# Conditioning bursts that wait for a fp32 product bundle, in one decoder layer on one core

## The chip, the cores and the metric

One core of one Trainium2 chip. The metric is device time in microseconds of one execution of the whole kernel. Engines are named as in the profile: PE is TensorE's matmuls (PEld its weight loads), DVE VectorE, ACT ScalarE, POOL GpSimd, SP the engine that issues most loads.

## What is computed

One layer (DEPTH is 1) of a conditioned decoder, for a prompt of 256 tokens and 8 samples of 8 tokens, 320 rows in all that share every weight. Cut to what matters here:

```python
mod = silu(c) @ w_ada + b_ada                      # conditioning: 6 sections of 2048
sh1, sc1, g1, sh2, sc2, g2 = split(mod, 6)
h = rmsnorm(x) * (1 + sc1) + sh1
q, k, v, og, u, ga, gb, alr = split(h @ w_in)
loga = log_sigmoid(alr @ w_a2 + b_a) / 16
o, s_new = gla(q, k, v, loga, s0)                  # recurrence, 4 heads, chunked
y_a = rmsnorm(o, gla_norm_g) * silu(og)
y_b = pool(u) * pool_scale                         # causal averages, then w_pool
x = x + g1 * ((sigmoid(ga) * y_a + sigmoid(gb) * y_b) @ w_o)
h2 = rmsnorm(x) * (1 + sc2) + sh2
x = x + g2 * ((silu(gate) * up) @ w_down)          # gate, up = split(h2 @ w_gu)
```

and a final norm. All weights and activations are fp32.

## The kernel before

**Projections.** Activations lie transposed, 16 tiles of 128 channels by 320 rows, each split into a high and a low part of a reduced fp32 kind (`hh`/`hl` ahead of the recurrence, `mh`/`ml` ahead of `w_o`). A weight tile is loaded (`raw`), its high part cast by ACT (`whi`, L160) and its low part taken by DVE (`wlo`, L161); five buffers of each. `mm3` then issues three matmuls: `whi` with the high part (L199), `whi` with the low part (L200), `wlo` with the high part (L201). I call these three a *step*. `proj` computes 256 columns in four *chunks* of four channel tiles, eight steps a chunk, 32 steps a *unit*. Units stand in two rotating accumulators (`ps`).

**Two kinds of other work stand between chunks.** At the end of each chunk `proj` calls two pumps.

- `ada_pump` adds a rate to a counter and, when it reaches one, calls `ada_step`: a *conditioning burst* of 32 fp32 matmuls (L252), each writing 32 of the 128 output partitions (a 32-column tile), with four loads of `w_ada` ahead and the next four behind. Every second burst ends a group: ACT copies it out (`adasb`), PE transposes it, DVE adds the bias. The rate is one burst in six chunks during the recurrence (24 in all up to the end of w_o), and about one in four during w_o.
- `gla_pump` does the same with `queue`, the list of the recurrence's *bundles* for the head whose projections have just been made. A bundle is a few functions of `gla_steps` called in one go (`together`): `s_gk` (gate products, fp32, L779/L780), `s_exp` (running sums, reduced fp32, L810/L811), `s_nat2`, `s_nat3`, `s_kp` (transposes), `s_attP` (sample scores, fp32, L955), `s_inter` (sample state read, fp32, 32-column tiles, L979), `s_state` (L1000), `s_att` (prompt scores, fp32, 32-column tiles, L879, and the 128-wide L884), `s_o` (L933/L935), `s_sfin` (L944), `s_norm` (column sum of squares, fp32, L1016, then root on ACT, reciprocal and scaling on DVE).

After the last head's bundles, `merge_step` gates the norm's result and adds the pooled branch (DVE, L1122 and L1123), `hilo` splits it into `mh12` to `mh15` (ACT) and `ml12` to `ml15` (DVE), and the w_o units read them in their fourth chunk. The units' first three chunks read only heads 0 to 2.

**What sets the order.** The code is written in one order; the compiler's scheduler then orders each engine's instructions by its own model of time, within the data's dependences and a few pinned places. The order of each engine is fixed before the run, and each engine works strictly in its order. So a call that moves in the code moves rows of several engines, some of them far away.

Of the kernel before, what the change touches and what calls it, by code (L numbers as in the profile page):

```python
# [82 lines left out]
def body(tc, A):  # L83
# [15 lines left out]
    def nm(s):  # L99
        uid[0] += 1  # L100
        return "%s_%d" % (s, uid[0])

    def misc():
        return pmisc.tile([P, 512], F32, tag="m", name=nm("pm"))
# [30 lines left out]
    def tr_exact(out, in_):  # L135

        PE.matmul(out, lhsT=in_, rhs=identr, start=True, stop=True)  # L137
# [44 lines left out]
    def split_chunk(src, nk, nn, key=None):  # L182

        if key in ready:
            k = 0
            for e in ready.pop(key):
                for j in range(e.h.shape[1]):
                    yield k, e.h[:, j], e.l[:, j]
                    k += 1
            return  # L190
        raw = asked.pop(key) if key in asked else raw_chunk(src, nk, nn)
        step = 512 // nn
        for k in range(0, nk, step):
            hi, lo = split(raw[:, k:min(k + step, nk)])
            for j in range(hi.shape[1]):
                yield k + j, hi[:, j], lo[:, j]

    def mm3(ps, whi, wlo, xhi, xlo, start, stop):
        PE.matmul(ps, lhsT=whi, rhs=xhi, start=start, stop=False)  # L199
        PE.matmul(ps, lhsT=whi, rhs=xlo, start=False, stop=False)  # L200
        PE.matmul(ps, lhsT=wlo, rhs=xhi, start=False, stop=stop)  # L201

    def proj(w, col, k0, k1, xh, xl):

        ps = pmain.tile([P, 2, 512], F32, tag="pm", name=nm("ps"))
        for c0 in range(k0, k1, 4):
            nk = min(4, k1 - c0)
            for j, whi, wlo in split_chunk(w[:, c0:c0 + nk, col:col + 256], nk, 256, (col, c0) if w is win else None):
                kt = c0 + j
                for i in range(2):  # L210
                    mm3(ps[:, i, :T], whi[:, i * P:(i + 1) * P], wlo[:, i * P:(i + 1) * P],
                        xh[kt], xl[kt], kt == k0, kt == k1 - 1)
            ada_pump()
            gla_pump()
        return ps

    def projs(wcols, k0, k1, xh, xl):
# [93 lines left out]
    ada_done = []  # L311
    ada_acc = [0.0, 0.0, 0]
# [2 lines left out]

        ada_acc[:] = [0.0, rate / 4, limit]

    def ada_pump():
        ada_acc[0] += ada_acc[1]
        if ada_acc[0] >= 1.0 and len(ada_done) < ada_acc[2]:  # L320
            ada_acc[0] -= 1.0
            ada_step()

    queue = []
    gla_acc = [0.0, 0.0]

    def gla_pump():

        gla_acc[0] += gla_acc[1]
        while gla_acc[0] >= 1.0:  # L330
            gla_acc[0] -= 1.0
            if queue:
                queue.pop(0)()

    def modp(sec, kt):
        return mod[:, sec * KT + kt, 0:1]
# [423 lines left out]
    def gla_steps(g):  # L760
# [3 lines left out]
        st = []  # L764
# [39 lines left out]
        def s_exp(d):  # L804
            def f():
                pa, pb = misc(), misc()
                ds = slice(d * P, (d + 1) * P)
                for ps, rows, s, rhs, a, b in ((pa, P, 0, M0, 0, NM0), (pa, TS, 2, MS, NM0, NM0 + NMS),
                                               (pb, P, 1, M1, 0, NM1)):
                    PE.matmul(ps[:, a:b], lhsT=E["lgh"][:rows, s, ds], rhs=rhs, start=True, stop=False)  # L810
                    PE.matmul(ps[:, a:b], lhsT=E["lgl"][:rows, s, ds], rhs=rhs, start=False, stop=True)  # L811
                EQ, EK, EX = E["EQ"][:, d], E["EK"][:, d], E["EX"][:, d]
                i16 = 1.0 / 16.0
                for dst, sc in ((EQ, i16), (EK, -i16)):
                    S.activation(dst[:, 0:P], pa[:, 0:P], AF.Exp, scale=sc)
                    S.activation(dst[:, P:2 * P], pb[:, 0:P], AF.Exp, scale=sc)
                    S.activation(dst[:, TP:T], pa[:, NM0:NM0 + TS], AF.Exp, scale=sc)
                S.activation(EX[:, 0:144], pa[:, P:NM0], AF.Exp, scale=i16)
                S.activation(EX[:, 144:416], pb[:, P:NM1], AF.Exp, scale=i16)
                S.activation(EX[:, 416:480], pa[:, NM0 + TS:NM0 + 2 * TS], AF.Exp, scale=i16)  # L820
            return f
# [142 lines left out]
        def s_load(gg, d):  # L964
            def f():
                t = lp.tile([P, 4, DV], F32, tag="S0", bufs=2, name=nm("S0"))
                nc.gpsimd.dma_start(t, A["state_gla"][0, 4 * gg:4 * gg + 4, h, d * P:(d + 1) * P, :]
                                    .rearrange("b p e -> p b e"))
                E["S0", gg, d] = t
            return f  # L970

        def s_inter(gg):
            def f():
                pt = E["oi"] = misc()
                PE.matmul(pt, lhsT=attP[:, gg], rhs=E["vp"][:, gg], start=True, stop=False,
                          skip_group_check=True)
                for d in range(2):
                    for j in range(4):
                        PE.matmul(pt[32 * j:32 * j + 32, :], lhsT=qeP[:, d, 4 * gg + j, :], rhs=E["S0", gg, d][:, j],  # L979
                                  start=False, stop=d == 1, tile_position=(0, 32 * j), skip_group_check=True)  # L980
            return f

        def s_oback(gg):
            def f():
                t = lp.tile([P, DV], F32, tag="sf", name=nm("osn"))
                S.copy(t, E["oi"])
                p2 = misc()
                for e in range(4):
                    tr(p2[:, e * P:(e + 1) * P], t[:, e * P:(e + 1) * P])
                src = p2.rearrange("p (e j t) -> p e j t", e=4, t=32)  # L990
                for e in range(4):
                    V.tensor_copy(s3(E["o"][:, e, TP + 32 * gg:TP + 32 * gg + 32]), src[:, e, :, 0:LS])
            return f
# [29 lines left out]
        def together(*fs):  # L1023
            def f():
                for x in fs:
                    x()
            return f

        def states(gg, d):
            return s_state(gg, d, 0), s_state(gg, d, 2)  # L1030

        st += [together(s_load(0, 0), s_load(0, 1), s_wa2), s_gk, together(s_exp(0), s_exp(1)),
               together(s_prod, s_vstack), together(s_nat2, s_nat3, s_kp(0)), s_attP, s_inter(0),
               together(s_oback(0), *states(0, 0), s_load(1, 0)), together(*states(0, 1), s_load(1, 1), s_att),
               together(s_nat, s_kp(1)), together(s_o(0), s_o(1), s_sfin(0), s_sfin(1)), s_inter(1),
               together(s_oback(1), *states(1, 0)), together(*states(1, 1)), s_norm]
        return st, E

    def pool_steps(g):
# [96 lines left out]
    st, E = gla_steps(g0)  # L1136
# [13 lines left out]
    for h in range(1, H):  # L1150
        g = new_group(h)
        for kind, i, col in units(h):
# [8 lines left out]
            if kind == "u":  # L1161
                pump(len(queue))
                st, E = gla_steps(g)
# [277 lines left out]
```

## Time and profile before

| what | value |
|---|---|
| median of 3 runs | 1951.73 us (1951.36 to 1951.95) |
| the profiled execution, own time | 1950.37 us |
| its span, first to last instruction | 1948.6 us |
| mean granted TensorE clock | 0.997 |
| TensorE busy | 1929.4 us, 99% |
| VectorE, ScalarE busy | 1015.9 us, 824.1 us |
| conditioning bursts from the recurrence to the end of w_o | 24 of 32 matmuls |

A row of the timeline gives the start (us from the span's start), the duration, the engine, the source line, what is written and read, and how many instructions were merged into the row. An fp32 instruction of TensorE shows as two records, so a burst of 32 reads x64. Matmuls overlap: a duration of 0.31 says little, and the distance from one start to the next is what a matmul costs. In the rows of stretches, each engine's busy time is followed by the granted clock (1.00 is full), the DMA share and GB/s.

### The profile page before, as it was taken

To read this page: it belongs to the slowest core of one execution; us is meant where nothing else is said; L and a number is where in the kernel's file an instruction comes from. 1 tells how busy PE (TensorE), PEld (TensorE's weight loads), DVE (VectorE), ACT (ScalarE), POOL (GpSimd) and SP (SyncE) were. 2 spreads that over 40 slices of the span, in tenths; PEclk is the share of its full clock that TensorE was granted. 3 is DMA by queue.
4 is the path that set the end of the run, shared out by engine and by line. 5 is a ranking of instruction groups with operands and counts; after the bars stand their busy time and mean duration, and the time that the engine had idled before them with its cause. 6 is when DMAs were issued, how large, how long until landed. Compare 5 with 4: busy or idle time off the path is not lost.

```text
span 1948.6 us, 37288 instructions
## 1 busy us (share of the span) xinstructions
PE 1929.4 (99%) x15060; PEld 1851.4 (95%) x15060; DVE 1015.9 (52%) x1909; ACT 824.1 (42%) x1482; POOL 135.8 (7%) x255
## 2 busy tenths in 40 slices
PE   9999999999999999999999999999999999999997
PEld 7899999899899989889999999999999999999997
DVE  3566565565466437666574444444444444444554
ACT  4333355355336333744353333343333334344443
POOL 1012210121002002010020000000000000000000
PEclk9999999999999999999999999999999999999998
DMA  9988555686786778589656655444444444444443
GB/s 323 398 275 266 191 167 173 228 294 212 272 272 203 228 260 279 179 288 327 222 188 207 218 189 178 152 146 152 146 153 151 152 152 152 148 148 149 150 137 103
DMA packets 324608, 400.84 MB, mean 206 GB/s; under 512 B 13546, under 2 KB 264682, under 8 KB 324098
## 3 DMA queue, kind: packets, MB, share of 16 engines
q1 hardware_dynamic: 312082, 357.95, 56.5%
q0 software_dynamic: 12272, 40.25, 5.8%
q8 instruction: 118, 1.93, 0.4%
q14 instruction: 56, 0.45, 0.1%
q10 hardware_dynamic: 80, 0.26, 0.0%
HBM read 373.96 MB, written 24.67 MB: 205 GB/s over the span
## 4 chain that ended last, share of the span: by engine, by line
PE 92%; DVE 1%; DMA 1%; ACT 0%; issue 0%; DVEq 0%; ACTq 0%
PE ps L199 28%; PE ps L200 27%; PE ps L201 27%; PE pm L252 4%; PE pm L979 1%; PE pm L1000 1%; PE pm L944 1%; PE pm L133 1%; DMA raw<-w_in 1%; PE pm L933 0%; PE pm L810 0%; PE psy L199 0%; PE pm L137 0%; PE psy L200 0%; PE psy L201 0%
## 5 line engine op out<-in xcount | busy, mean ns | idle before, releaser
L161 DVE TENSOR_TENSOR wlo<-raw,whi 128x512 fp32r<-128x512 f32 x948 | 652.7, 692 | 751.6 <-ACT whi L160 749.3
L160 ACT CAST whi<-raw 128x512 fp32r<-128x512 f32 x948 | 583.8, 620 | 936.2 <-PE ps L200 864.7
L199 PE MATMUL ps<-hh,whi 128*128 128x320 f32 x1408 | 443.8, 316 | 2.5 <-ACT hh L585 1.0
L200 PE MATMUL ps<-hl,whi 128*128 128x320 f32 x1408 | 437.0, 311 | 0.7 <-DVE hl L601 0.7
L201 PE MATMUL ps<-hh,wlo 128*128 128x320 f32 x1408 | 436.6, 310 | 0.1
L200 PE MATMUL ps<-h2l,whi 128*128 128x320 f32 x1408 | 434.8, 309 | 0.8 <-DVE h2l L1291 0.8
L199 PE MATMUL ps<-h2h,whi 128*128 128x320 f32 x1408 | 435.2, 310 | 0.0
L201 PE MATMUL ps<-h2h,wlo 128*128 128x320 f32 x1408 | 434.8, 309 | 0.0
L199 PEld LDWEIGHTS ps<-hh,whi 128*128 128x128 f32 x1408 | 264.7, 188 | 22.7 <-issue 15.3
L200 PEld LDWEIGHTS ps<-hl,whi 128*128 128x128 f32 x1408 | 265.0, 188 | 4.5 <-issue 1.8
L201 PEld LDWEIGHTS ps<-hh,wlo 128*128 128x128 f32 x1408 | 265.0, 188 | 1.9 <-issue 0.9
L199 PEld LDWEIGHTS ps<-h2h,whi 128*128 128x128 f32 x1408 | 264.1, 188 | 1.6 <-ACT ah L348 1.4
L200 PEld LDWEIGHTS ps<-h2l,whi 128*128 128x128 f32 x1408 | 264.3, 188 | 1.1 <-DVE h2l L1291 1.1
L201 PEld LDWEIGHTS ps<-h2h,wlo 128*128 128x128 f32 x1408 | 264.3, 188 | 0.0
L201 PE MATMUL ps<-ah,wlo 128*128 128x320 f32 x704 | 218.1, 310 | 0.0
L200 PE MATMUL ps<-al,whi 128*128 128x320 f32 x704 | 217.6, 309 | 0.0
L199 PE MATMUL ps<-ah,whi 128*128 128x320 f32 x704 | 217.5, 309 | 0.0
L199 PEld LDWEIGHTS ps<-ah,whi 128*128 128x128 f32 x704 | 132.2, 188 | 0.0
L201 PEld LDWEIGHTS ps<-ah,wlo 128*128 128x128 f32 x704 | 132.2, 188 | 0.0
L200 PEld LDWEIGHTS ps<-al,whi 128*128 128x128 f32 x704 | 132.2, 188 | 0.0
L252 PE MATMUL pm<-raw,scT 128*32 128x128 f32 (+1 forms) x2688 | 95.9, 290 | 0.0
L252 PEld LDWEIGHTS pm<-raw,scT 128*32 128x32 f32 x2688 | 72.7, 110 | 17.1 <-issue 9.2
(327 smaller groups left out, 1565.6 us busy)
## 6 DMA issues: line engine op xcount, KB each, us to landing
raw<-w_ada SPq DMA_DIRECT2D x192, 512.0 KB, 7.4
raw<-w_gu SPq DMA_DIRECT2D x176, 512.0 KB, 3.5
raw<-w_in SPq DMA_DIRECT2D x173, 512.0 KB, 4.2
raw<-w_down SPq DMA_DIRECT2D x79, 512.0 KB, 3.3
S<-state_gla POOLq DMA_DIRECT2D x16, 1024.0 KB, 8.1
o_gs<-S POOLq DMA_DIRECT2D x16, 1024.0 KB, 6.1
raw<-w_o SPq DMA_DIRECT2D x32, 512.0 KB, 6.3
raw<-w_down SPq DMA_DIRECT2D x15, 256.0 KB, 2.5
```

What stands on the lines that cost most here:

```text
L133: PE.transpose(out, in_, ident[:k, :k])
L160: S.copy(hi, raw)
L161: V.tensor_sub(lo, raw, hi.bitcast(F32))
L199: PE.matmul(ps, lhsT=whi, rhs=xhi, start=start, stop=False)
L200: PE.matmul(ps, lhsT=whi, rhs=xlo, start=False, stop=False)
L201: PE.matmul(ps, lhsT=wlo, rhs=xhi, start=False, stop=stop)
L252: ins = PE.matmul(ps[32 * j:32 * j + 32, 0:w], lhsT=scT[:, k, :], rhs=raws[j], start=k == 0 if start is None else start, stop=k == KT - 1 ...
L944: PE.matmul(pt, lhsT=E["kdn"][:, s, d * P:(d + 1) * P], rhs=E["vn"][:, s], start=s == 0, stop=s == 1)
L979: PE.matmul(pt[32 * j:32 * j + 32, :], lhsT=qeP[:, d, 4 * gg + j, :], rhs=E["S0", gg, d][:, j], start=False, stop=d == 1, tile_position=(0 ...
L1000: PE.matmul(pt, lhsT=kpz[:, j, d * P:(d + 1) * P], rhs=E["vp"][:, gg], start=True, stop=True)
```

## The change

Four edits, all in what is issued when; no arithmetic changes.

- At the end of a chunk `proj` calls `gla_pump` ahead of `ada_pump`.
- A burst that is due while `queue` holds bundles waits until it is three chunks late, unless a bundle marked as ending in an fp32 product is issued: then it is issued directly behind that bundle (`ada_due`, `full`, `last`).
- Nine of the fifteen bundles are marked so.
- Two bundles are turned round, so that they end in fp32 transposes: `s_nat2, s_kp(0), s_nat3` and `s_kp(1), s_nat`.

```diff
             gla_pump()
             ada_pump()
-            gla_pump()
...
+    def ada_due(late):
+        if ada_acc[0] >= 1.0 + late * ada_acc[1] and len(ada_done) < ada_acc[2]:
+            ada_acc[0] -= 1.0
+            ada_step()
+
     def ada_pump():
         ada_acc[0] += ada_acc[1]
-        if ada_acc[0] >= 1.0 and len(ada_done) < ada_acc[2]:
-            ada_acc[0] -= 1.0
-            ada_step()
+        ada_due(3 if queue else 0)
...
             if queue:
-                queue.pop(0)()
+                step = queue.pop(0)
+                step()
+                if step in full:
+                    ada_due(0)
...
-               together(s_prod, s_vstack), together(s_nat2, s_nat3, s_kp(0)), s_attP, s_inter(0),
+               together(s_prod, s_vstack), last(together(s_nat2, s_kp(0), s_nat3)), last(s_attP), last(s_inter(0)),
...
-               together(s_oback(1), *states(1, 0)), together(*states(1, 1)), s_norm]
+               together(s_oback(1), *states(1, 0)), together(*states(1, 1)), last(s_norm)]
```

Lines behind the first edits shift by 9 to 13: L1016 of before is L1025 in the changed file, L879 is L888, L933 is L942, L1018 is L1027.

In the order of TensorE, of the bursts issued while a head's bundles are pending or just done, three stand directly behind or among 32-column products before and three in the change; behind 128-wide fp32 products or transposes one before, six in the change. Three places are shown, with row names as the order gives them.

First, TensorE around the norm's column sum of head 3, in w_o (ps_1592 is unit 1, ps_1568 unit 0, mh3 a tile of head 0, mh11 the last of head 2, mh12 the first of head 3). Before:

```order
L199 MATMUL ps_1592_10098<-mh3_9846,whi_1596_10117 128x320
L1016 MATMUL pm_1559_9784<-acc_1557_9777,cst_76 128x320
L200 MATMUL ps_1592_10098<-ml3_9862,whi_1596_10117 128x320
L201 MATMUL ps_1592_10098<-mh3_9846,wlo_1597_10118 128x320
L199 MATMUL ps_1592_10098<-mh3_9846,whi_1596_10117 128x320
```

and in the change:

```order
L200 MATMUL ps_1592_10098<-ml11_9870,whi_1612_10230 128x320
L1025 MATMUL pm_1554_9743<-acc_1552_9736,cst_76 128x320
L201 MATMUL ps_1592_10098<-mh11_9854,wlo_1613_10231 128x320
L252 MATMUL pm_1555_9751<-raw_1501_9464,scT_86 32x128 x8
L252 MATMUL pm_1555_9751<-raw_1500_9462,scT_86 32x128 x8
L252 MATMUL pm_1555_9751<-raw_1499_9460,scT_86 32x128 x8
L252 MATMUL pm_1555_9751<-raw_1498_9458,scT_86 32x128 x8
L199 MATMUL ps_1568_9947<-mh12_9855,whi_1585_10052 128x320
L199 MATMUL ps_1592_10098<-mh12_9855,whi_1615_10248 128x320
L200 MATMUL ps_1568_9947<-ml12_9871,whi_1585_10052 128x320
```

The sum stood 16 steps, a burst and a transpose ahead of the first row that reads mh12; now one projection matmul and a burst stand between.

Second, ScalarE at the same place: weight splits (whi), the table load and root of the norm, and the casts of head 3's merged tiles (mh). Before:

```order
L160 CAST whi_1607_10196<-raw_1604_10178 128x512
L1018 ACT_TABLE_LOAD
L1018 ACTIVATE acc_1557_9777<-pm_1559_9784,epst_81 128x320
L160 CAST whi_1610_10214<-raw_1609_10212 128x512
L305 COPY adasb_1602_10173<-pm_1537_9665 128x128
```

and in the change:

```order
L160 CAST whi_1617_10264<-raw_1614_10246 128x512
L160 CAST whi_1625_10299<-raw_1624_10297 128x512
L1027 ACT_TABLE_LOAD
L1027 ACTIVATE acc_1552_9736<-pm_1554_9743,epst_81 128x320
L357 CAST mh12_9855<-mg3_114 128x320
```

All weight splits that units 0 and 1 need, and one of unit 2 (whi_1625), now stand ahead of the root, and nothing between the root and the cast of mh12.

Third, TensorE at head 0's output products (v_15 are the values, transposed into pm_636 and copied by ACT into w4_635). Before:

```order
L199 MATMUL ps_649_4255<-hh4_95,whi_657_4302 128x320
L200 MATMUL ps_649_4255<-hl4_1197,whi_657_4302 128x320
L933 MATMUL pm_643_4230<-attT_3226,w4_634_4176 128x256
L935 MATMUL pm_643_4230<-attT_3226,w4_634_4176 128x128
L933 MATMUL pm_643_4230<-attT_3226,w4_634_4176 128x256
```

and in the change:

```order
L133 MATMUL pm_628_4138<-identr_78,adasb_627_4136 128x128
L137 MATMUL pm_634_4176<-identr_78,w4_537_3601 128x128 x2
L133 MATMUL pm_636_4184<-identr_78,v_15_250 128x128 x4
L133 MATMUL pm_637_4190<-identr_78,v_15_250 128x128 x4
L942 MATMUL pm_643_4230<-attT_3226,w4_635_4183 128x256
L942 MATMUL pm_644_4236<-attT_3226,w4_635_4183 128x256
L199 MATMUL ps_649_4255<-hh0_91,whi_651_4258 128x320
```

The first output products moved up to directly behind the transposes whose copy they read.

More of the change, by code (lines that the diff above doesn't have):

```diff
@@ L212, in proj @@
                         xh[kt], xl[kt], kt == k0, kt == k1 - 1)
+            gla_pump()
             ada_pump()
-            gla_pump()
         return ps
@@ L316, in ada_rate @@
         ada_acc[:] = [0.0, rate / 4, limit]
+    def ada_due(late):
+        if ada_acc[0] >= 1.0 + late * ada_acc[1] and len(ada_done) < ada_acc[2]:
+            ada_acc[0] -= 1.0
+            ada_step()
     def ada_pump():
         ada_acc[0] += ada_acc[1]
-        if ada_acc[0] >= 1.0 and len(ada_done) < ada_acc[2]:
-            ada_acc[0] -= 1.0
-            ada_step()
+        ada_due(3 if queue else 0)
     queue = []
     gla_acc = [0.0, 0.0]
+    full = []
     def gla_pump():
@@ L1030, in states, with last @@
             return s_state(gg, d, 0), s_state(gg, d, 2)
-        st += [together(s_load(0, 0), s_load(0, 1), s_wa2), s_gk, together(s_exp(0), s_exp(1)),
-               together(s_prod, s_vstack), together(s_nat2, s_nat3, s_kp(0)), s_attP, s_inter(0),
-               together(s_oback(0), *states(0, 0), s_load(1, 0)), together(*states(0, 1), s_load(1, 1), s_att),
-               together(s_nat, s_kp(1)), together(s_o(0), s_o(1), s_sfin(0), s_sfin(1)), s_inter(1),
-               together(s_oback(1), *states(1, 0)), together(*states(1, 1)), s_norm]
+        def last(f):
+            full.append(f)
+            return f
+        st += [together(s_load(0, 0), s_load(0, 1), s_wa2), last(s_gk), together(s_exp(0), s_exp(1)),
+               together(s_prod, s_vstack), last(together(s_nat2, s_kp(0), s_nat3)), last(s_attP), last(s_inter(0)),
+               together(s_oback(0), *states(0, 0), s_load(1, 0)), last(together(*states(0, 1), s_load(1, 1), s_att)),
+               last(together(s_kp(1), s_nat)), last(together(s_o(0), s_o(1), s_sfin(0), s_sfin(1))), last(s_inter(1)),
+               together(s_oback(1), *states(1, 0)), together(*states(1, 1)), last(s_norm)]
         return st, E
```

## The prediction

> **What bounds the kernel now.** I read the page first, then who waited for whom on TensorE, then TensorE's rows in order of time around every conditioning burst and bundle.
>
> ```profile
> PE 1929.4 (99%) x15060; PEld 1851.4 (95%) x15060; DVE 1015.9 (52%) x1909; ACT 824.1 (42%) x1482; POOL 135.8 (7%) x255
> ...
> PE pm L137 <- DVE w L859: 1.2, 1, 1.2
> ...
> 1200.00:1300.00 100.00, 100.00 (x684) 99.99 (x683) 43.42 (x64) 39.33 (x64) 0.00 (x0) 1.00 0.47 146
> ```
>
> TensorE has a row open for 99% of the span; its longest wait in the stretch that the change touches is 1.2 us, once. A stretch of pure projection holds 684 matmuls in 100 us, so one starts every 0.146 us and a step (three matmuls) takes 0.44 us. Nothing is waiting to be uncovered: the time moves only if TensorE loses less at its joints, or if something new is late for it.
>
> **What a joint costs.** First a burst alone between projection matmuls:
>
> ```profile
> 603.75 0.31 PE L201 MATMUL ps<-hh,wlo 128*128 128x320 f32 x1
> 603.99 1.96 PE L252 MATMUL pm<-raw,scT 128*32 128x128 f32 x64
> 605.87 0.41 PE L199 MATMUL ps<-hh,whi 128*128 128x320 f32 x1
> 606.12 0.30 PE L200 MATMUL ps<-hl,whi 128*128 128x320 f32 x1
> ```
>
> The burst starts 0.24 us after the last projection matmul, 0.09 late, and the second one behind it is 0.10 late. From 603.75 to 606.12 less two ordinary spacings, a burst costs 2.08 us. Next, the score products (32-column tiles, as a burst has) alone, then with a burst behind them, then with the 128-wide L884 behind them:
>
> ```profile
> 829.82 0.31 PE L201 MATMUL ps<-hh,wlo 128*128 128x320 f32 x1
> 830.06 0.31 PE L879 MATMUL pm<-w,EQK 128*32 128x128 f32 x3
> ...
> 830.88 0.31 PE L200 MATMUL ps<-hl,whi 128*128 128x320 f32 x1
> 831.03 0.61 PE L884 MATMUL pm<-w,EX 128*128 128x128 f32 x4
> ...
> 831.62 0.31 PE L199 MATMUL ps<-hh,whi 128*128 128x320 f32 x1
> ...
> 686.13 0.31 PE L201 MATMUL ps<-hh,wlo 128*128 128x320 f32 x1
> ...
> 686.83 1.93 PE L252 MATMUL pm<-raw,scT 128*32 128x128 f32 x64
> ...
> 688.94 0.31 PE L200 MATMUL ps<-hl,whi 128*128 128x320 f32 x1
> ...
> 681.68 0.31 PE L200 MATMUL ps<-hl,whi 128*128 128x320 f32 x1
> ...
> 683.19 0.31 PE L199 MATMUL ps<-hh,whi 128*128 128x320 f32 x1
> ```
>
> Less two spacings each: score products alone 0.77, L884 alone 0.45. With a burst behind them 2.52 instead of 0.77 + 2.08, so 0.33 is saved. With L884 behind them 1.22 = 0.77 + 0.45: nothing is saved, though both are fp32. What the joint costs goes by the width of the tiles here, not by the number format.
>
> **The change, part by part.** No instruction is added or removed on TensorE; only the order differs.
>
> 1. *Bursts beside 32-column products* (score L879, state read L979). By the order there are three before and three in the change. 0.
>
> 2. *Bursts beside 128-wide fp32 products* (gate L779/L780, L944, L955, L1016, transposes): one before, six in the change. No row shows a burst behind such a product. Bounds for five: 0 (as L884 behind L879) and -1.65 us (0.33 each). Being nearest to the L884 row, I take 0.1 each, -0.5.
> The Trainium skill, "TensorEngine Tiling (Array Packing)", section Key Properties, says that changing the tiling mode, not just the tile, drains TensorE. By that rule a burst behind a 128-wide product drains as it does behind a projection, and this part is worth 0 instead of -0.5; by number format it would be -1.65. The three stretches above agree with the rule; no run here shows this very pair.
>
> 3. *The wait of 1.2 us* for the stacked values of head 3 (L137, at 803.9): in the change the transposes stand 16 steps (7 us) behind the last gate-exponent product, where before 7 steps and a burst (5.2 us) lay between. The wait goes, -1.2; if not, 0.
>
> 4. *The other groups* of the bundles are cut and joined anew (a burst split in two before and again after, head 0's second half of the score products no longer alone, head 3's state read now in two pieces). I priced every group in the order by the row of the same group before; the sum over the stretch differs by -0.6, with +-1 for groups that have no such row.
>
> 5. *Head 3's norm.* This is the term that decides. The bundles of head 3 now pass behind the score products later, and the norm's column sum (L1016, L1025 in the changed file) stands behind all 48 steps of w_o units 0 and 1 that do without head 3; before, some 16 steps, a burst and a transpose still followed it. What hung on it before:
>
> ```profile
> 867.45 0.62 ACT L160 CAST whi<-raw 128x512 fp32r<-128x512 f32 x1 [1.55 <-PE ps L200]
> 868.08 1.28 ACT L1018 ACT_TABLE_LOAD   x1
> 868.42 0.70 PE L1016 MATMUL pm<-acc,cst 128*128 128x320 f32 x2
> 869.38 0.53 ACT L1018 ACTIVATE acc<-pm,epst 128x320 f32<-128x320 f32 x1
> 869.94 2.15 DVE L1019 RECIPROCAL acc<-acc 128x320 f32<-128x320 f32 x1 [1.15 <-ACT acc L1018]
> 872.55 1.93 DVE L1021 SCALAR_TENSOR_TENSOR EQK<-EQK,vec,acc 128x320 f32<-128x320 f32 x4
> 874.40 1.69 DVE L1122 TENSOR_TENSOR EQK<-EQK,og 128x320 f32<-128x320 f32 x4
> 876.61 0.88 DVE L1123 TENSOR_TENSOR mg<-EQK,mg 128x320 f32<-128x320 f32 x2
> 877.13 0.46 ACT L348 CAST mh<-mg 128x320 fp32r<-128x320 f32 x1 [1.05 <-DVE mg L1123]
> 878.92 0.48 DVE L349 TENSOR_TENSOR ml<-mg,mh 128x320 fp32r<-128x320 f32 x1
> 878.93 0.46 PE L199 MATMUL ps<-mh,whi 128*128 128x320 f32 x2
> 879.46 0.41 PE L200 MATMUL ps<-ml,whi 128*128 128x320 f32 x1
> ```
>
> From the sum's start to the first use of ml12 were 11.0 us, and TensorE worked through 10.5 of them: the first mh12 matmul stands where the 48 steps end, and only about 0.25 us was lost before ml12. In the change, count from the sum's start t0. The last split that ACT owes (whi_1625) needs the buffer freed by the matmul just ahead of t0: it starts at about t0 + 0.2 and takes 0.62; the table load 1.28, the root 0.53 (t0 + 2.7). The reciprocal takes 2.1 to the next start, the scaling 1.85, the gating 1.6 (t0 + 8.2). mh12 is cast 0.52 after the first merge starts and takes 0.46 (t0 + 9.2); all four merges now stand ahead of ml12 on DVE, 1.6, then 0.48 (t0 + 10.4). TensorE has for cover the sum itself, one projection matmul and one burst: 0.7 + 2.08, free at t0 + 2.8. It waits 6.5 us for mh12, does two matmuls, and waits 0.8 more for ml12: 7.3, less the 0.25 of before, +7.0. Bounds: +6.2 (ACT's split not in the way) and +8 (the chain as slow as before). Behind it are the end of both units, the next burst, and the residuals; the loads gain by it.
>
> 6. *The clock after that wait.* Twice before the granted clock fell:
>
> ```profile
> 33.00:34.00 1.00, 0.98 (x6) 0.80 (x6) 0.90 (x3) 0.65 (x2) 0.14 (x1) 0.87 0.65 251
> 34.00:35.00 1.00, 1.00 (x5) 1.00 (x5) 1.00 (x2) 0.00 (x0) 0.00 (x0) 0.50 0.84 221
> 35.00:36.00 1.00, 1.00 (x6) 1.00 (x5) 0.69 (x2) 0.32 (x1) 0.00 (x0) 0.50 0.75 131
> 36.00:37.00 1.00, 1.00 (x5) 1.00 (x5) 0.07 (x1) 0.90 (x2) 0.00 (x0) 0.50 0.82 238
> 37.00:38.00 1.00, 1.00 (x8) 1.00 (x8) 0.62 (x1) 0.12 (x1) 0.00 (x0) 0.92 0.99 291
> ...
> 1938.00:1939.00 1.00, 0.22 (x2) 0.00 (x0) 0.80 (x3) 0.74 (x2) 0.00 (x0) 0.69 0.00 0
> ```
>
> After the thin work at 30 us it was 0.50 for some 3.4 us of dense matmuls, which lost 0.13 + 1.5 + 0.08 = 1.7 us. At the end it fell at about 1938.4 (0.69 over that microsecond), within about 3 us of the end of the stream. An idle stretch of 6.5 us should bring it down: +1.7; bounds 0 (no fall) and +3.4 (two such stretches).
>
> 7. *Head 0's first output products* (L933) now stand directly behind the transposes of v, where a copy by ACT comes between; before, 26 steps lay between.
>
> ```profile
> 363.63 0.58 ACT L895 COPY w<-pm 128x512 f32<-128x512 f32 x1 [0.17 <-PE pm L133]
> ...
> 881.30 7.75 SPq L1180 DMA_DIRECT2D x<-xspill  x16
> ...
> raw<-w_ada SPq DMA_DIRECT2D x8, 512.0 KB, 8.7
> ```
>
> The copy takes 0.58 and starts some 0.3 behind the transposes, with 0.44 us of other transposes as cover: +0.5; bounds 0 and +1.1 (one 0.62 us split ahead of it on ACT).
>
> 8. *The burst behind next*, in unit 2 of w_o. Its four w_ada loads stand on SP's queue behind the 16 reloads of x, which wait for head 3's last ml (7.75 us of issue), and wait themselves for the burst just ahead, 21 steps (9.2 us) earlier; they took 8.7 us to land. +0.4; bounds 0 and +2. Everywhere else, loads come at least a burst's distance of 10 us or more ahead: 0.
>
> Sum: 0 - 0.5 - 1.2 - 0.6 + 7.0 + 1.7 + 0.5 + 0.4 = +7.3 us. The profiled execution took 1950.37 us (span 1948.6), so 1957.7 in its terms; the median of the runs is 1951.73, 1.4 above it, and gives **1959.0 us**, 0.37% slower. Under 0.2%, 3.9 us, a difference can hardly be told from none.
>
> **Rivals.** *The clock holds* through the wait: +5.6, 1957.3, still slower. Against it are the two falls above. *The norm's wait is half of that*, because ACT's table load or split comes earlier and the merges interleave as before: +2 to +3.8, about 1954.7, no change by the bound. Against it: the reciprocal, the scaling and the gating alone are 5.5 us on one engine and cannot overlap. *Faster:* the sum is read early enough that no wait arises, so only terms 2 to 4 are left with the full 0.33 for each of the five joined bursts: -1.65 - 1.2 - 1.6 = -4.5, 1947.2. It decides only if the chain from the sum to mh12 takes under 3 us; the reciprocal alone takes 2.15. *Slower still:* the chain takes the 11 us of before, two clock stretches and the late w_ada loads come together: +11 to +13, about 1963.
>
> **How the numbers follow.** Forecast (norm wait with the clock's fall) 0.64; clock holds 0.12; half a wait 0.13; faster 0.04; slower still 0.07. Slower by over 0.2% is the first, second and last, 0.83; same 0.13; faster 0.04. All low ends together give 1953.4 (-1.65 - 1.2 - 1.6 + 6.2), all high ends 1966; I give 1954 to 1963, which leaves out the faster case and the worst sums.
>
> **What would show it.** TensorE's first mh12 matmul waits 6 to 8 us, about 10 us behind L1025; the granted clock is at 0.50 there and for some 3 us on; a wait near 0.5 us at head 0's first output product; no 1.2 us wait at head 3's value transposes; burst with L1025 or L780 ahead of it costs close to 2.08. I am wrong if mh12 comes within 5 us of the sum, or if TensorE waits anywhere else for more than 2 us.

## Result and profile after

| | before | changed |
|---|---|---|
| median | 1951.55 us (1951.21 to 1951.95, 4 runs) | 1971.68 us (1970.39 to 1976.1, 4 runs) |
| profiled execution | 1950.37 us | 1970.39 us |
| ratio | | 1.0107 (1.0095 to 1.0119) |

The change makes the kernel 20 us slower, where 7.3 us were forecast and 1963 us was the range's upper end. (The ratio is worked out over all runs; it is not the quotient of the two medians.) The changed kernel's page, its span and its busy engines:

```profile
span 1968.6 us, 37287 instructions
...
PE 1932.7 (98%) x15060; PEld 1852.2 (94%) x15060; DVE 1020.0 (52%) x1909; ACT 823.9 (42%) x1480; POOL 137.5 (7%) x255
```

The work of TensorE is the same, 15060 instructions. What is new are waits. From TensorE's list of waits (what it waited for, us in total, times, longest), the long ones that the list of before does not have (for whi it has one wait, of 0.5):

```profile
PE ps L199 <- ACT mh L357: 6.6, 1, 6.6
PE pm L252 <- DMA raw<-w_ada: 3.8, 2, 3.5
PE ps L199 <- ACT whi L160: 2.6, 2, 2.1
...
PE pm L133 <- POOL cm L1076: 1.9, 1, 1.9
...
PE pm L988 <- DMA S<-state_gla: 0.9, 1, 0.9
```

The first is the forecast one. The others are transfers and a copy that the forecast costed at nothing or at 0.4 us. To place the 20 us I compared the two timelines at the same projection step, with 2.08 us taken off for each burst that one kernel had done more; the figures hold to about 0.3 us. The changed kernel is behind by 1.3 us at step 520 (ahead of anything the change moves; the other kernels below lie between -0.1 and +2.9 there, so this is the run), by 6.1 at step 1350 (the end of heads 0 to 2), 4.5 at step 1480, 14.0 at step 1512 and 19.9 from step 1530 to the end. At step 1480 it still has to do the norm's sum, one state update and one transposition that the kernel before has done by then; by their rows they cost 0.55, 0.23 and 0.11 us, so 0.9 of the 9.5 us from there to step 1512 is work that was only put off. So: **heads 0 to 2 +4.8, head 3's bundles -0.7, the norm +8.6, the w_ada loads of w_o +5.9.**

The norm's chain in the changed kernel, rows of four engines in order of time:

```profile
879.57 0.70 PE L1025 MATMUL pm<-acc,cst 128*128 128x320 f32 x2
880.34 1.96 PE L252 MATMUL pm<-raw,scT 128*32 128x128 f32 x64
881.70 0.53 ACT L1027 ACTIVATE acc<-pm,epst 128x320 f32<-128x320 f32 x1
882.26 2.15 DVE L1028 RECIPROCAL acc<-acc 128x320 f32<-128x320 f32 x1 [1.06 <-ACT acc L1027]
884.44 1.94 DVE L1030 SCALAR_TENSOR_TENSOR EQK<-EQK,vec,acc 128x320 f32<-128x320 f32 x4
888.43 1.66 ACT L357 CAST mh<-mg 128x320 fp32r<-128x320 f32 x4 [6.20 <-DVE mg L1136]
888.94 0.90 PE L199 MATMUL ps<-mh,whi 128*128 128x320 f32 x2 [6.64 <-ACT mh L357]
890.06 0.63 PE L200 MATMUL ps<-ml,whi 128*128 128x320 f32 x1 [0.22 <-DVE ml L358]
```

From the sum to mh12 are 9.4 us, to ml12 10.5, with the burst as the only cover. The granted clock (third column from the end) falls in that wait, and again in the next one:

```profile
886.00:888.00 2.00, 0.00 (x0) 0.00 (x0) 2.00 (x6) 0.00 (x0) 0.00 (x0) 0.50 1.05 407
...
892.00:894.00 2.00, 2.00 (x14) 2.00 (x13) 0.00 (x0) 0.15 (x1) 0.00 (x0) 0.85 0.33 82
...
908.00:910.00 2.00, 0.00 (x0) 0.00 (x0) 0.00 (x0) 0.00 (x0) 0.00 (x0) 0.92 1.06 393
910.00:912.00 2.00, 0.81 (x16) 0.77 (x20) 0.00 (x0) 0.00 (x0) 0.00 (x0) 0.50 1.09 385
```

The second one is the burst at step 1521, two bursts behind the norm. SP's queue and TensorE there (of the burst's 64 records the last row holds the first 16):

```profile
891.28 8.97 SPq L1193 DMA_DIRECT2D x<-xspill  x16
900.35 2.40 SPq L150 DMA_DIRECT2D raw<-w_ada  x4
...
907.43 0.31 PE L200 MATMUL ps<-ml,whi 128*128 128x320 f32 x1
911.19 1.08 PE L252 MATMUL pm<-raw,scT 128*32 128x128 f32 x16 [3.45 <-DMA raw<-w_ada]
```

The reloads of x could start only when the last ml had been made, at 891. They held the queue to 900.25, and the w_ada loads behind them were issued until 902.75, with the DMA share at 1.05 to 1.09. They were there at 911.2; TensorE stood from 907.7.

### The profile page after: what moved, and what is told of

Its sections match the earlier page's. It is cut to its first block, busy times and chain, and to the rows that moved or that the text cites. A ratio compares the mean times of both kernels' runs of the same rounds, so it can differ in the third digit from the quotient of the medians.

```text
span 1968.6 us, 37287 instructions
## 1 busy us (share of the span) xinstructions
PE 1932.7 (98%) x15060; PEld 1852.2 (94%) x15060; DVE 1020.0 (52%) x1909; ACT 823.9 (42%) x1480; POOL 137.5 (7%) x255
## 4 chain that ended last, share of the span: by engine, by line
PE 89%; DMA 2%; issue 1%; DVE 1%; POOL 1%; ACT 0%; DVEq 0%; POOLq 0%; ACTq 0%
PE ps L199 27%; PE ps L200 27%; PE ps L201 27%; PE pm L252 4%; DMA raw<-w_in 1%; PE pm L988 1%; PE pm L1009 1%; PE pm L133 1%; PE pm L953 1%; DMA raw<-w_ada 0%; DMA S<-state_gla 0%; PE pm L819 0%; PE pm L942 0%; POOL cm L1076 0%; PE pm L137 0%
```

## Experiments

Each is compared with the kernel before on the same chip. Waits are of the profiled execution.

| run | edit | median us | ratio to before (95%) |
|---|---|---|---|
| h3_old | change, head 3 by the old rules, bundles still turned | 1964.02 | 1.0059 (1.0047 to 1.0072) |
| h3_new | change for head 3 alone, bundles of all heads turned | 1964.94 | 1.0062 (1.0050 to 1.0075) |
| swap_only | pump order alone | 1960.70 | 1.0045 (1.0032 to 1.0059) |
| no_lateness | change without lateness | 1960.43 | 1.0045 (1.0033 to 1.0057) |
| turned_only | two bundles turned alone | 1958.99 | 1.0038 (1.0025 to 1.0052) |
| change_unturned | change without the turn | 1969.54 | 1.0087 (1.0074 to 1.0100) |
| late_norm | before, head 3's bundles spread wider | 1967.98 | 1.0087 (1.0073 to 1.0101) |
| close_bursts | before, w_o's bursts moved | 1958.46 | 1.0041 (1.0028 to 1.0053) |
| wo_spread | change, w_o's bursts spread | 1964.90 | 1.0072 (1.0060 to 1.0085) |
| fill_wait | wo_spread, norm's wait filled | 1965.33 | 1.0067 (1.0054 to 1.0081) |
| chain_pinned | wo_spread, norm tile by tile | 1969.08 | 1.0089 (1.0074 to 1.0104) |
| cm_own | wo_spread, cm in another buffer | 1965.11 | 1.0058 (1.0045 to 1.0071) |
| h3_old_unturned | h3_old, head 3 unturned | 1961.01 | 1.0039 (1.0024 to 1.0054) |
| repaired | all named places undone | 1952.91 | 1.0005 (0.9996 to 1.0015) |

### Head 3 alone, heads 0 to 2 alone

```diff
-            gla_pump()
-            ada_pump()
+            if old[0]:
+                ada_pump()
+                gla_pump()
+            else:
+                gla_pump()
+                ada_pump()
...
-        ada_due(3 if queue else 0)
+        ada_due(3 if queue and not old[0] else 0)
...
+                old[0] = h == 3
```

In h3_new the last line is `old[0] = h != 3`. No burst is issued behind a marked bundle while `old[0]` holds, and the two bundles of every head stay turned in both.

> The changed kernel, but from head 3's bundles on with the old rules (burst ahead of bundle, no lateness, nothing marked). The norm's sum of head 3 then stands at step 1472 as before (1471), not at 1488, and the bursts of w_o at 1472, 1512, 1544. Theory (three separate places: heads 0 to 2 lose about 4 us in new waits for loads, head 3's norm about 9 with the clock, the w_ada loads of w_o about 6 with a second clock fall): 1955.7 us, between 1954 and 1957.5, no wait for mh12 over 0.5 us, no w_ada wait in w_o, but still the waits for whi near 760 us, for cm near 411 and for the state near 382. Rival (the late bursts starve the loads everywhere, head 3 is only where it is seen): above 1961. Rival (heads 0 to 2 cost nothing): 1951.5.

> The counterpart: the old rules for heads 0 to 2, the new ones from head 3's bundles on (sum of head 3 at step 1488, bursts of w_o at 1488, 1500, 1522, 1551). Theory: 1951.5 + 15 = 1966.5 us, 1965 to 1968; a wait of 6 to 7 us for mh12, 3 to 4 us for w_ada, both with a half clock behind. The two kernels' differences from before add up to the change's 20 us within 1 us if the places are separate. Rival (the whole state of the load queue matters, so the parts do not add): the sum of the two differences is off by more than 3 us.

h3_new: 1964.9 (profiled 1961.48), 1.6 below the forecast and just below its range: 6.64 for mh12 with the clock's fall, but 2.10 for w_ada without one. **h3_old missed:** 1964.0 instead of 1955.7 (1957.5 at most), so the two differences, 12.0 and 12.9, add to 5 more than the change's 20, and by the test written down the parts do not add. Heads 0 to 2 cost it 5.2 us by step 1350, as in the change. But head 3 then lost 7.6 us more between steps 1430 and 1446:

```profile
860.95 1.94 PE L993 MATMUL pm<-S,qeP 128*32 128x512 f32 x8 [3.66 <-DMA S<-state_gla]
```

a wait for head 3's states with the clock at 0.50 behind it (a matmul there took 1063 ns; 592 is the median). Neither the kernel before nor the change has that wait, and the theory had no term for it.

### The pump order alone

```diff
-            ada_pump()
             gla_pump()
+            ada_pump()
```

> The kernel before with one edit: bundles ahead of bursts in each chunk, no lateness, nothing marked, nothing turned round. The sum of head 3 stands at step 1478, a burst at 1488. Theory: the chain from the sum to mh12 (9.4 us) meets 10 steps (4.4), the burst (2.1) and the sum itself (0.7): a wait of about 2 us for mh12 and up to 0.8 for ml12, no fall of the clock, no w_ada wait, and little else, since the bursts stay evenly spaced: 1954 us, 1952 to 1956. Rival (pump order is what costs heads 0 to 2 their 4 us): 1957 to 1960.

1960.7, a miss (1952 to 1956 forecast). In its profiled execution (1956.67) mh12 did not wait at all, because something else did ahead of it: the burst at step 1488, 1.88 us for w_ada, and at half clock.

```profile
880.02 3.59 PE L252 MATMUL pm<-raw,scT 128*32 128x128 f32 x64 [1.88 <-DMA raw<-w_ada]
```

Between steps 600 and 800 it lost 2.0 us, the change 2.8: most of that part of heads 0 to 2 comes with the pump order. 1.42 of the 2.0 is a wait for cm in head 0, whose sum stands at step 660 here, at 655 in before and at 665 in the change.

### The bursts of w_o

```diff
     ada_rate(0.94, 24)
+    ada_acc[0] = -1.0      # wo_spread, on the change
+    ada_acc[0] = 0.25      # close_bursts, on the kernel before
```

> The changed kernel with the burst counter of w_o started at -1, so that the bursts behind the norm stand at steps 1488, 1512, 1544 (24 and 32 steps apart) instead of 1488, 1500, 1521, 1551; the burst left over is issued at step 1653. Nothing else moves. Theory (the loads of the burst at 1521 came late because it stood 21 steps behind one that itself stood 12 behind another): the 3.5 us wait for w_ada and the half clock behind it go, the mh12 wait of 6.6 us stays: 1971.5 - 6 = 1965.5 us, 1964 to 1967.5. Rival (the loads are behind the x reloads, whichever burst it is): a wait of 2 us or more at the burst at 1512 or 1544 and 1969 or more.

> The kernel before with the burst counter of w_o started at 0.25 instead of 0: the bursts there stand at steps 1440, 1500, 1523, 1553 (in the change 1488, 1500, 1521, 1551) instead of 1440, 1472, 1512, 1544. The norm's sum stays at 1471, but no burst stands between it and mh12. Theory (two bursts 23 steps apart behind the x reloads are enough): a wait of 1 to 2.5 us for mh12 and one of 2 to 4 us for w_ada at the burst at 1523, with or without a fall of the clock: 1952.2 + 4 to 8 = 1958.5 us, 1956 to 1961. Rival (w_ada was late only because the norm's wait pushed the x reloads against it): no wait over 1 us at that burst, 1952 to 1955.

Both came out as forecast. wo_spread: 1964.9, the w_ada wait is gone, 6.64 for mh12 is left; from step 1512 to 1530 it loses 0.2 us, the change 5.9. close_bursts: 1958.5, with 1.95 us of wait for mh12 and, in a kernel without any other edit, this:

```profile
905.67 1.96 PE L252 MATMUL pm<-raw,scT 128*32 128x128 f32 x64 [3.26 <-DMA raw<-w_ada]
```

So the distance between bursts behind the x reloads is the cause, and it needs no late norm.

### The norm's wait

late_norm changes `SPREAD = (8, 10, 4)` to `(8, 10, 7)` in the kernel before.

> The kernel before with one number changed: head 3's bundles are spread over 7 units instead of 4, so what is left of them is issued at the end of the queue and the norm's sum stands at step 1488, as in the change, while the bursts of w_o stay at 1472, 1512 and 1544. Heads 0 to 2 are as before. Theory (the late sum alone costs its chain): no burst behind the sum, so the wait for mh12 is about 8.5 us (9.3 less the sum's 0.7), the clock falls, no w_ada wait, nothing late near 382, 411 or 760: 1952.2 + 8.7 + 2.0 = 1963 us, 1961 to 1965. Rival (the norm's wait only shows because loads are late as well): under 1957.

```profile
885.15 1.44 PE L1016 MATMUL pm<-acc,cst 128*128 128x320 f32 x2 [3.33 <-DVE acc L1014]
893.86 0.90 PE L199 MATMUL ps<-mh,whi 128*128 128x320 f32 x2 [7.06 <-ACT mh L348]
```

1968.0, 5 above the forecast and outside its range: the wait is there and costs more, because the sum itself also waited 3.3 us for VectorE, and the state update 0.8. The clock fell in the sum's wait and stayed at 0.50 for 13.7 us, through the wait for mh12. Heads 0 to 2 and w_ada lost nothing. A late sum costs without any late load.

fill_wait, on wo_spread, for head 3 between the root and the reciprocal:

```diff
             S.activation(rs, pt[:, 0:T], AF.Sqrt, scale=1.0 / DV, bias=epst)
+            for _ in range(34 if h == 3 else 0):
+                PE.matmul(pt[:, 0:DK], lhsT=identr, rhs=kpz[:, 0, :], start=True, stop=True)
             V.reciprocal(rs, rs)
```

> The kernel with the spread bursts of w_o, and in the wait for mh12 34 matmuls of 256 columns that compute nothing used (they write the sum's PSUM tile once the root has read it). mh12 is no earlier: 9.2 to 9.7 us behind the sum. Theory (the half clock is a price of the idle stretch, by itself 2.4 us: 16 matmuls 0.267 apart instead of 0.147, and a little): granted clock 1.00 from the sum on, waits of at most 2.5 us ahead of the fillers and 1 us at mh12, 1964.9 - 2.4 = 1962.5 us, 1961.5 to 1963.5. Rival (the clock falls there for another reason, such as the load traffic or the fp32 products): still 0.50 behind mh12, and 1964.9.

```profile
881.37 4.31 PE L1029 MATMUL pm<-kpz,identr 128*128 128x256 f32 x34 [1.86 <-ACT acc L1027]
888.04 0.56 PE L199 MATMUL ps<-mh,whi 128*128 128x320 f32 x2 [0.47 <-ACT mh L357]
...
895.97 0.48 DVE L1207 SCALAR_TENSOR_TENSOR x<-ps,mod,x 128x256 f32<-128x256 f32 x1 [1.95 <-DMA x<-xspill]
897.25 0.39 PE L199 MATMUL ps<-mh,whi 128*128 128x320 f32 x1 [1.09 <-DVE rt L1210]
```

The clock stayed at 1.00 from the sum on, so the idle stretch alone brings it down. But the time did not fall (1965.3, where at most 1963.5 was forecast): from step 1480 to 1530 this kernel loses 9.3 us, wo_spread 9.6. Between steps 1488 and 1500 it loses 0.4 us and wo_spread 2.6, but by step 1512 it has lost 1.4 more and wo_spread nothing. The faster matmuls met the next limit: the residual of unit 0 needs the reloaded x, and unit 2 waits for its accumulator.

chain_pinned, on wo_spread: head 3's scaling is moved out of `s_norm` into `merge_step`, tile by tile, and `pin` keeps these instructions of head 3 in the order of the code (the lines of `merge_step`):

```diff
             for e in range(4):
                 o = E["o"][:, e]
+                if g.h == 3:
+                    pin(V.scalar_tensor_tensor(o, o, GNG[:, e:e + 1], E["rs"], op0=ALU.mult, op1=ALU.mult))
-                V.tensor_tensor(o, o, g.og[:, e], op=ALU.mult)
-                V.tensor_tensor(g.gb[:, e], o, g.gb[:, e], op=ALU.add)
+                pin(V.tensor_tensor(o, o, g.og[:, e], op=ALU.mult))
+                pin(V.tensor_tensor(g.gb[:, e], o, g.gb[:, e], op=ALU.add))
```

> The kernel with the spread bursts of w_o; on VectorE head 3's scaling, gating and merge are issued tile by tile instead of four scalings, four gatings, four merges. Same instructions, same sum at step 1488. Theory (the wait is the chain's length and nothing else): mh12 comes 6.6 to 7.0 us behind the sum instead of 9.4, its wait is 4.0 instead of 6.6, the clock still falls: 1964.9 - 2.6 = 1962.3 us, 1961.3 to 1963.3; 1960 if the shorter wait leaves the clock up. Rival (mh12 waits for ACT or for the loads, not for this chain): 1964.9.

```profile
884.61 0.90 PE L199 MATMUL ps<-mh,whi 128*128 128x320 f32 x2 [4.36 <-ACT mh L357]
897.25 0.39 PE L199 MATMUL ps<-mh,whi 128*128 128x320 f32 x1 [2.40 <-DVE rt L1214]
```

The wait fell by 2.3 us as the chain got shorter: the chain is its cause. The time did not fall. The median is 1969.1, and the profiled execution, the fastest of five, took 1965.2 and loses 12.0 us from step 1480 to 1530: the last ml now came later on VectorE (the x reloads started at 892.0 instead of 890.1), the same residual was late by 2.4, and the clock fell a second time. What made the other four executions longer still is not shown. Both misses say the same: behind the norm stands the reload of x, and what is gained ahead of it is given back.

### Head 0

```diff
-            cm = lp.tile([P, 2, TS], F32, tag="acc", name=nm("cm"))
+            cm = lp.tile([P, 2, TS], F32, tag="dh", name=nm("cm"))
```

> The kernel with the spread bursts of w_o; the pooling history's copy (cm, on POOL) takes the buffer of dh instead of the buffer of the norm's sum. Theory (the 1.9 us wait near 411 is head 0's norm, met ten steps later than before, through that shared buffer): the wait is gone or under 0.5 us, and 1964.9 - 1.9 = 1963.0 us, 1962 to 1964. Rival (POOL's copy is late by its own 5 us, or TensorE waits for the next thing there): a wait of over 1 us stays near 411 and the time is 1964.9.

The wait at 411 is gone. Its cause stands in these rows, of the change and then of before:

```profile
404.38 1.94 DVE L1030 SCALAR_TENSOR_TENSOR EQK<-EQK,vec,acc 128x320 f32<-128x320 f32 x4
406.46 5.16 POOL L1076 COPY cm<-u 128x64 f32<-128x64 f32 x2 [3.48 <-DVE EQK L1030]
411.50 0.30 PE L133 MATMUL pm<-identr,cm 128*64 128x128 f32 x1 [1.86 <-POOL cm L1076]
```

```profile
400.13 1.93 DVE L1021 SCALAR_TENSOR_TENSOR EQK<-EQK,vec,acc 128x320 f32<-128x320 f32 x4
402.20 3.76 POOL L1063 COPY cm<-u 128x64 f32<-128x64 f32 x2 [0.57 <-DVE EQK L1021]
407.37 0.27 PE L133 MATMUL pm<-identr,cm 128*64 128x128 f32 x1
```

The copy takes over the norm's buffer, so it starts when head 0's scaling is done, and the norm's sum stands ten steps later in the change than before. The copies themselves also took 1.4 us longer, so not all of the 1.86 is the later start; in cm_own they do not stand behind the norm, and both go. The time, 1965.1, is not the 1963 forecast. In that execution the states of head 0 were 1.46 us late and the weights at 758 2.46, with a half clock behind the latter; wo_spread's had 0.47 and no wait at 758, but a half clock behind its wait for cm. These waits differ from run to run: for the states of head 0 the profiles of the same order of instructions have anything from none to 3.7 us.

### Marks, lateness, turn

no_lateness: `ada_due(3 if queue else 0)` becomes `ada_due(0)`.

> The changed kernel without the lateness: a due burst never waits three chunks, but bundles come first, nine are marked and two are turned round. The sum of head 3 stands at step 1479 and the bursts of w_o at 1470, 1488, 1512, nearly as with the pump order alone. Theory (lateness puts the norm at the end of the 48 steps, bunches the bursts and makes whi late near 760; marks and turns do next to nothing): as the pump order alone, 1960.5 us, 1958.5 to 1962; no wait for mh12 over 2 us, none at 760. Rival (burst behind 128-wide fp32 products is what costs): within 4 us of the change's 1971.5.

1960.4, as the pump order alone, as forecast, with no wait for mh12 and none at 760. It had 4.6 us for w_ada at step 1488, which the expectation did not name: that burst stands 18 steps behind the one at 1470, its loads were issued from 867.9 to 873.4, and it started at 883.3. This fits the distance between bursts again, as in the pump order alone (18 steps, 1.88), and here the x reloads come only behind it (889.8); no run moves that burst alone. Lateness carries the late norm and the weights at 760; marks and bursts behind fp32 products do nothing that shows in the time.

turned_only:

```diff
-together(s_nat2, s_nat3, s_kp(0))
+together(s_nat2, s_kp(0), s_nat3)
...
-together(s_nat, s_kp(1))
+together(s_kp(1), s_nat)
```

> The kernel before with the change's fourth edit alone: the two bundles are turned round so that they end in fp32 transposes. The order of bursts and of the norm moves by at most 4 steps (norm at 1472, a burst at 1444). Every theory: no difference, 1952.2 us, 1951.2 to 1953.2; more than 1.5 us would mean that the turn itself makes something late.

**1959.0: every theory was wrong.** Of the 7.4 us that this execution is behind before at the end, 6.0 are one wait, 3.90 us for head 3's states, with the clock's fall; 0.9 is a wait for ml12. Rows of turned_only:

```profile
823.40 1.63 DVE L349 TENSOR_TENSOR ml<-mg,mh 128x320 fp32r<-128x320 f32 x1 [1.67 <-ACT mh L348]
825.35 2.05 DVE L1002 SCALAR_TENSOR_TENSOR S<-S,dec,pm 128x512 f32<-128x512 f32 x3
829.73 0.73 DVE L1002 SCALAR_TENSOR_TENSOR S<-S,dec,pm 128x512 f32<-128x512 f32 x1
...
830.76 0.84 POOL L1004 DMA_DIRECT2D o_gs<-S  x1 [6.08 <-DVE S L1002]
837.82 0.77 POOL L967 DMA_DIRECT2D S<-state_gla  x1 [6.22 <-DMA o_gs<-S]
...
850.22 0.79 POOL L967 DMA_DIRECT2D S<-state_gla  x1 [7.02 <-DMA o_gs<-S]
856.30 1.14 PE L979 MATMUL pm<-S,qeP 128*32 128x512 f32 x8 [3.90 <-DMA S<-state_gla]
```

and of before:

```profile
825.41 0.74 DVE L1002 SCALAR_TENSOR_TENSOR S<-S,dec,pm 128x512 f32<-128x512 f32 x1
826.45 0.84 POOL L1004 DMA_DIRECT2D o_gs<-S  x1 [2.31 <-DVE S L1002]
831.86 0.77 POOL L967 DMA_DIRECT2D S<-state_gla  x1 [4.56 <-DMA o_gs<-S]
...
842.99 0.75 POOL L967 DMA_DIRECT2D S<-state_gla  x1 [9.62 <-DMA o_gs<-S]
```

Two buffers hold the states: updated by VectorE, stored by POOL, reloaded when the store has landed, read by TensorE. The first store waits for four updates. In the turned kernel all four stand behind the first split ml on VectorE, which waits 1.67 for ACT; in before three of them stand ahead of that split (820.8 to 823.5). The fourth and the first store go 4.3 us later, the second reload 7.2 (0.7 of both is the run's lag), and the read, which in before came 6.7 us after its load was issued (it landed after 5.5), waits.

> The changed kernel without its fourth edit (bundles unturned). Norm's sum at step 1488 and bursts at 1488, 1500, 1521 as in the change. Theory (in the change head 3's state read stands later and does not wait, so the turn costs little there): 1971.5 us within 2.5, mh12 wait 6.6, w_ada wait 2 to 4. Rival (the turn costs its 6 to 7 us here too): 1965.

1969.5 (profiled 1968.78), 6.64 for mh12 and 4.43 for w_ada: the time is as forecast, the w_ada wait 0.4 above its 2 to 4. In the change itself the turn costs at most about 2 us, the difference of the two medians, not 7: head 3's states are read later there, and neither of the two kernels waits for them.

### All places undone

> As the run with head 3 by the old rules, but head 3's two bundles are also back in their old order (that run had kept them turned). On VectorE the fourth state update of head 2 then stands ahead of the split ml8 again, as before. Theory (the 3.7 us wait for head 3's states, and the half clock behind it, come from the turned bundles alone, through that VectorE order and the store and reload of the state buffer): no wait over 0.5 us for the states of head 3, 1964.0 - 7 = 1957 us, 1955.5 to 1959. What is left over before is heads 0 to 2. Rival (heads 0 to 2, 5 us late, make the states late): the wait stays and 1961 or more.

> The changed kernel with each place undone that the runs have named: head 3 by the old rules and unturned, no lateness for heads 0 to 2, cm in the buffer of dh. What stays of the change: bundles ahead of bursts and bursts behind marked bundles in heads 0 to 2. Theory (nothing else costs): 1953.0 us, 1951.5 to 1955, no wait over 1.2 us on TensorE outside the start. Rival (a burst behind 128-wide fp32 products costs by itself, or the moved bundles do): 1956 or more. A gain on the kernel before (under 1951.4) would be the joints' saving, which no trace has shown.

h3_old_unturned: the wait for head 3's states is gone, and from step 1350 to 1512 the kernel loses 0.7 us (h3_old 8.0). So the place is confirmed, but the time is a miss: the median, 1961.0 (1956.8 to 1964.0), is 3 us below h3_old where 7 were forecast. Its profiled execution is the slowest of them, with 3.69 us for head 0's states and the half clock behind that. repaired: 1952.9 against 1951.5, no difference that can be measured. The two longest waits that are left in the recurrence:

```profile
381.58 1.07 PE L993 MATMUL pm<-S,qeP 128*32 128x512 f32 x8 [0.67 <-DMA S<-state_gla]
805.73 0.41 PE L137 MATMUL pm<-identr,w 128*128 128x128 f32 x2 [1.25 <-DVE w L873]
```

It keeps the pump order and the marks for heads 0 to 2, so these gain nothing either. No version was faster than the kernel before.

## Why the prediction was right and wrong

By place, the forecast had -1.8 for head 3's bundles (terms 3 and 4), +8.7 for the norm with the clock (terms 5 and 6), +0.4 for the w_ada loads and nothing for heads 0 to 2 but term 7's +0.5 and its part of terms 2 and 4. Measured are -0.7, +8.6, +5.9 and +4.8, and 1.3 that this execution was behind from the start. The deciding mechanism came as forecast; what was missing lies elsewhere. The prediction's own sign of being wrong, a wait of over 2 us anywhere else, came twice (3.45 for w_ada, 2.15 at 760). Its rival "slower still" had the late w_ada loads and a second fall of the clock, at 0.07, but not heads 0 to 2. All high ends of its terms add to +14.9, so to 1966.6 (the prediction says 1966), still 5 us under the result: two terms were outside their bounds, not only off.

- **Term 5, the norm: right.** Forecast: mh12 9.2 us behind the sum, ml12 10.4, waits 6.5 and 0.8. Measured: 9.4, 10.5, 6.64 and 0.22. The filled and the pinned kernel confirm chain and idle stretch as causes. That shortening it gains nothing was not foreseen: the reload of x limits the same place.
- **Term 6, the clock: right.** +1.7 forecast. Behind mh12, TensorE's projection matmuls fell 2.07 us behind their usual distance of 0.146 until the clock was back at 892.6; less the wait of 0.22 for ml12 this is 1.85.
- **Term 8, the w_ada loads: the step that failed.** +0.4 forecast with 2 as its bound; 5.9 measured, 3.45 of wait and about 2.4 of half clock. The prediction saw the loads on SP's queue behind the x reloads, but set 8.7 us of landing against 9.2 us of steps. It left out that the reloads hold the queue until 2.2 us after the burst ahead has ended (898.05), that the four issues take 2.4 us more, and that a wait of that length halves the clock.
- **"Everywhere else, loads come at least a burst's distance of 10 us or more ahead: 0": the other step that failed.** Heads 0 to 2 cost 4.8. The waits there are 1.9 for head 0's cm behind the norm, 0.9 for states and 2.2 for weights at 760, whose loads stand behind four of w_ada on SP's queue. Only the TensorE order around bursts was priced there; the norm's delay of ten steps in head 0, a chain that ends late as in term 5, was not looked for.
- **Term 2: inside its bounds.** Bursts behind 128-wide products now have rows, the sum of head 1 with a burst in the change and alone in before:

```profile
543.69 0.31 PE L200 MATMUL ps<-hl,whi 128*128 128x320 f32 x1
543.84 0.70 PE L1025 MATMUL pm<-acc,cst 128*128 128x320 f32 x2
544.47 1.96 PE L252 MATMUL pm<-raw,scT 128*32 128x128 f32 x64
...
546.61 0.31 PE L199 MATMUL ps<-hh,whi 128*128 128x320 f32 x1
```

```profile
542.04 0.31 PE L199 MATMUL ps<-hh,whi 128*128 128x320 f32 x1
542.19 0.70 PE L1016 MATMUL pm<-acc,cst 128*128 128x320 f32 x2
...
542.88 0.30 PE L201 MATMUL ps<-hh,wlo 128*128 128x320 f32 x1
```

  Less two spacings the sum costs 0.55 alone and 2.63 with the burst: 0.55 + 2.08, nothing saved. This agrees with the Trainium skill, "TensorEngine Tiling (Array Packing)", section Key Properties, that a change of tiling mode drains TensorE. Behind the gate products of head 3 (1.83 alone, 3.71 with the burst) 0.20 was saved, which that rule alone does not give.
- **Terms 3 and 7: right, term 4 not shown.** The 1.2 us wait for head 3's stacked values is not in the change (it is, with 1.24 or 1.25, in every run with head 3 by the old rules and spread as before); head 0's first output product waits 0.24 behind its transposes. But steps 1350 to 1480 gained 0.7 where terms 3 and 4 had 1.8, so nothing shows of term 4's 0.6. Term 1 was not tried alone.
- The fourth edit was part of terms 2 and 4 and costed at nothing beside them. In the change it costs 2 us at most; alone it costs 7 us.

What stays open: why the loads of head 0's states and the weights at 760 are late by amounts that differ from run to run. A third buffer for the states, which might take their wait away, was not tried. Also open is why the same wait for cm brings the clock down in some executions and not in others.

## What to carry to other kernels

A kernel whose bound engine never waits may have no slack left behind it: list for each moved block the chains that end in it (update, store, reload; sum, root, scaling, cast; loads behind other loads on one queue) and compare each with the distance that the new order leaves, on the queues and on VectorE as well as on TensorE. Where the DMA share is already 1.0, as it was here, look at any two bursts of loads that move closer together. Count a wait of more than 3 us with the half clock behind it, hold it possible from about 2 us on, and try each edit alone, also the one that looks like nothing.

## What the hardware showed beside that

- The granted clock fell to 0.50 in, or at most 0.9 us behind, all but one of the TensorE waits of 3.26 us or more that began at full clock in these runs (3.33, 3.45, 3.66, 3.69, 3.90, 4.36, 4.43, 4.56 and every 6.64; not 3.26). Shorter ones went either way, and not by their length: the wait of 1.86 for cm brought it down in fill_wait, wo_spread and h3_old_unturned, but not in the change, chain_pinned and change_unturned; 1.88, 2.40 and 2.46 brought it down, 2.10, 2.17 and 2.28 did not. Each stretch at half clock lasted about 3.4 us or two, three or four times that (6.8, 10.2, 13.7). The two burst rows above (3.59 us behind 1.88 of wait, 1.96 behind 3.26) show the price. The Trainium skill, "TensorE: Matmul & The Clock Gate", Part 1, gives a free-running window of about 3.4 us and a fall after at least one idle window. The long waits and the lengths of the stretches agree; the falls at 1.86 to 2.46 do not fit a whole idle window.
- Two POOL copies of 128x64 took 5.16 us at 406 and 3.76 in before, nearly all of it the first (4.99 and 3.58); the median of this copy is 0.24. VectorE ran two-input rows on SBUF without a break beside both first copies, and each copy ended within 0.1 us of them (411.45 and 411.35, 405.78 and 405.69). What slows the copy is not tested.
